# An encoder block in one program: value sums begin with the last key block, and four kinds of small TensorE work are queued behind later dense products

## The chip, the core and the metric

The kernel runs on one core of one Trainium2 chip. The metric is the device time of one execution in microseconds. A core has TensorE (matmuls, called PE in the profile, with weight loads as PEld), VectorE (DVE), ScalarE (ACT), GpSimd (POOL) and SyncE (SP), which here only issues transfers. Each engine works through its own queue in order, and the queues meet in semaphores. All matrix work goes through TensorE; its results land in PSUM banks, from which VectorE and ScalarE read them.

## The reference, cut to what matters

One layer of an encoder over 2048 tokens of width 1024:

```python
h = rms_norm(x, pre_mix_g);  proj = h @ w_in
q, k, v = split(proj[..., :1536])              # 8 heads of 64
y_a = chunk_band_attention(q, k, v, rel_bias)  # chunks of 64, own chunk + 8 before
y_b = rwkv7_time_mix(proj[..., 1536:3328], ...)
merged = sigmoid(gate_a) * (y_a @ proj_a) + sigmoid(gate_b) * (y_b @ proj_b)
x = x + rms_norm(merged @ w_out, post_mix_g)
u = square(relu(rms_norm(x, pre_ffn_g) @ w_up)) @ w_down
x = x + rms_norm(u, post_ffn_g)

# inside rwkv7_time_mix, one step per token:
sa = einsum('bhij,bhj->bhi', state, -kk)
state = state * w + sa[..., None] * (kk * a) + v[..., None] * k
y = einsum('bhij,bhj->bhi', state, r)
# then a group norm of y, "+ bonus", and "* (sigmoid(cg) @ g2)", the gate product
```

Everything is in float32. The order in which the attention sums its key blocks is not fixed by the reference.

## The kernel before, in words

Each float32 operand is split into a high part that TensorE takes at its fast rate (fp32r) and a low remainder, and a product is three matmuls: high by high, high by low, low by high. `wsplit` and `split` (L69 to L83) do it: a weight block of 512 KB is loaded by SP into a raw buffer, ScalarE casts the high part `whi` (L80), VectorE subtracts to get the low part `wlo` (L81). A raw buffer is loaded again when L81 has read it.

The tokens go through in four groups of 512 (g = 0 to 3). A group has three stages: the time mixing (`phase_rwkv`), the attention (`phase_attention`), and the merge of the branches. The feed-forward part follows, two groups at a time. TensorE's filler everywhere is the dense product `dense`: one column block of `w_in`, 24 matmuls of 128x512, named `psd`. 14 of them make the inputs of the time mixing and 16 the branch gates, so a group's time mixing has 30 (matmuls 0 to 719 of a list `self.dl`), and each head pair of the attention has three, for q, k and v. The attention of a group works through four head pairs.

In the time mixing the heads go in four pairs p = 0 to 3, in two blocks of two. For a block: `rwkv_pre` prepares decays and scores (`ps_A`, `ps_bk`, `ps_bonus`); `rwkv_inverse` forms a triangular inverse `X` on VectorE in 31 steps of two short instructions (L593, L599) and two transposes (L602, L604); `rwkv_blocks` (L624, L632) takes `X` to TensorE; `rwkv_trans` makes a transition matrix per chunk of 64 tokens; and `recurrence` walks over the eight chunks. A chunk of a pair (`rwkv_chunk`) is two state products `ps_st` (L710), two output products `ps_y` (L714), and the new state `ST` on VectorE (L715). Both products read the state of the chunk before. When all chunks are done, `rwkv_post` normalises the output: squares on ScalarE, a sum on VectorE, a power on GpSimd, the product `yn` on VectorE (L733). Its second part transposes `yn` back in two halves (`ps_yt`, L742), evicts them with scale and bias on ScalarE (L744, L747), and multiplies by the gate product `ps_g` (three matmuls). While the second block's `X` steps run on VectorE, TensorE does dense products and the first block's `rwkv_post`.

In the attention, q and k of a head pair are taken from their `psd` banks by ScalarE and VectorE (L904 to L915) into `QA`, `QB` and `KK`; `KK` and `VV` hold the group before too, which SP loads from memory (L896, L897) where g > 0. For each head and each half of the queries there are two query blocks: scores `ps_s` against up to 640 keys in two pieces (L958), a minimum on VectorE (L964), the exponential on ScalarE (L971), transposes `ps_pt` (L977), and their split into `PTh` and `PTl` (L981, L982). The value sum `ps_pv` (L988) then adds twelve matmuls: `PTh` with key blocks kt = 0 to 5, `PTl` with the same. Block kt = 5 is filled by the second query block only, kt = 0 by the first only. The residual of the group before is worked off beside the first head pairs (`residual`, loads `o_prev` and `xr`, L1175).

What sets the order: a scheduler puts the instructions into each engine's queue by the order of the code and by their dependencies. In the time mixing, some TensorE instructions carry a further dependency without a semaphore, "behind matmul number n of the list of dense matmuls": `place` notes the pair and `placed` applies it with `queue_behind`. The numbers stand at the head of the file. The other engines' queues, SP's too, follow from the same schedule.

## Time and profile before

| | us |
|---|---|
| median of 3 timed runs (3223.13 to 3225.56) | 3224.54 |
| span of the profiled execution | 3228.5 |
| TensorE busy in it | 3169.8 |
| VectorE busy | 2239.4 |
| ScalarE busy | 1576.3 |

The span is from the first to the last instruction of one execution, which ran 4.0 us longer than the median. A row of a timeline has the start in us, the length in us, the engine, the line, the operation, what it writes and reads, its shape and how many equal ones are merged; in square brackets stand the idle time ahead of it and what ended it. A wait on TensorE shows as such a bracket.

### The profile page before, as it was taken

To read this page: it belongs to the slowest core of one execution; us is meant where nothing else is said; L and a number is where in the kernel's file an instruction comes from. 1 tells how busy PE (TensorE), PEld (TensorE's weight loads), DVE (VectorE), ACT (ScalarE), POOL (GpSimd) and SP (SyncE) were. 2 spreads that over 40 slices of the span, in tenths; PEclk is the share of its full clock that TensorE was granted. 3 is DMA by queue.
4 is the path that set the end of the run, shared out by engine and by line. 5 is a ranking of instruction groups with operands and counts; after the bars stand their busy time and mean duration, and the time that the engine had idled before them with its cause. 6 is when DMAs were issued, how large, how long until landed. Compare 5 with 4: busy or idle time off the path is not lost. (4 is left out here: it accounts for less than half of the span.)

```text
span 3228.5 us, 49999 instructions
## 1 busy us (share of the span) xinstructions
PE 3169.8 (98%) x18913; PEld 2592.1 (80%) x18913; DVE 2239.4 (69%) x3655; ACT 1576.3 (49%) x2511; POOL 602.6 (19%) x1101
## 2 busy tenths in 40 slices
PE   8999999999999999999999999999999999999998
PEld 6877778877888877888877888888888878888887
DVE  7785666786776785776866775887656668765464
ACT  5435635445744435745434755545543454544343
POOL 2222012132112222102222110121211112210000
PEclk9999999999999999999999999999999999999999
DMA  5345374257574237564336557654787876456565
GB/s 169 86 134 184 125 241 123 71 161 245 170 248 121 82 122 246 177 225 151 95 104 222 167 180 272 202 183 153 279 275 251 284 236 209 159 169 235 196 219 172
DMA packets 432282, 592.54 MB, mean 184 GB/s; under 512 B 25300, under 2 KB 295840, under 8 KB 432040
## 3 DMA queue, kind: packets, MB, share of 16 engines
q1 hardware_dynamic: 373928, 408.94, 40.4%
q0 software_dynamic: 48896, 163.61, 13.8%
q10 hardware_dynamic: 9216, 16.78, 1.4%
q8 instruction: 149, 2.44, 0.3%
q14 instruction: 93, 0.76, 0.1%
HBM read 425.37 MB, written 167.01 MB: 183 GB/s over the span
## 5 line engine op out<-in xcount | busy, mean ns | idle before, releaser
L1438 PE MATMUL ps_dn<-fop 128*128 128x512 f32 x2688 | 611.0, 389 | 0.6 <-DVE fop L81 0.6
L1438 PEld LDWEIGHTS ps_dn<-fop 128*128 128x128 f32 x2688 | 504.3, 188 | 105.3 <-DVE fop L81 1.0
L80 ACT CAST whi<-wraw 128x1024 fp32r<-128x1024 f32 x232 | 243.5, 1049 | 331.6 <-PE psd L90 236.3
L90 PE MATMUL psd<-hh,whi 128*128 128x512 f32 x1344 | 369.0, 402 | 1.1 <-ACT k L373 1.1
L81 DVE TENSOR_TENSOR wlo<-wraw,whi 128x1024 fp32r<-128x1024 f32 x232 | 283.1, 1220 | 121.8 <-ACT whi L80 61.9
L90 PE MATMUL psd<-hh,wlo 128*128 128x512 f32 x1344 | 360.6, 397 | 0.0
L90 PE MATMUL psd<-hl,whi 128*128 128x512 f32 x1344 | 357.8, 396 | 0.0
L90 PEld LDWEIGHTS psd<-hl,whi 128*128 128x128 f32 x1344 | 247.5, 188 | 48.9
L90 PEld LDWEIGHTS psd<-hh,whi 128*128 128x128 f32 x1344 | 245.3, 190 | 50.5 <-ACT k L373 1.6
L90 PEld LDWEIGHTS psd<-hh,wlo 128*128 128x128 f32 x1344 | 246.0, 188 | 48.3
L81 DVE TENSOR_TENSOR fop<-xraw,fop 128x1024 fp32r<-128x1024 f32 x112 | 137.0, 1224 | 175.0 <-ACT fop L80 174.4
L80 ACT CAST fop<-xraw 128x1024 fp32r<-128x1024 f32 x112 | 117.8, 1051 | 246.1 <-PE ps_dn L1438 192.2
L1308 POOL DMA_DIRECT2D xd<-X x192 | 104.1, 543 | 379.2 <-ACT X L1305 313.2
L81 DVE TENSOR_TENSOR fop<-wdraw,fop 128x1024 fp32r<-128x1024 f32 x112 | 136.6, 1220 | 21.8 <-ACT fop L80 21.6
L80 ACT CAST fop<-wdraw 128x1024 fp32r<-128x1024 f32 x112 | 117.6, 1050 | 39.9 <-DMA wdraw<-in_w_down_dram 24.7
L964 DVE CUSTOM_DVE_ANT_0 sc<-bias,ps_s 128x640 f32<-128x640 f32 (+4 forms) x128 | 93.9, 734 | 48.6 <-PE ps_s L958 26.6
L971 ACT ACTIVATE sc<-sc,mn 128x640 f32<-128x640 f32 (+4 forms) x128 | 97.7, 763 | 27.7 <-DVE mn L964 26.2
L982 DVE TENSOR_TENSOR PTl<-ps_pt,PTh 128x640 fp32r<-128x640 f32 (+4 forms) x128 | 94.5, 738 | 24.0 <-ACT PTh L981 22.5
L80 ACT CAST s12h<-s 128x1024 fp32r<-128x1024 f32 x32 | 33.7, 1054 | 154.6 <-PE ps_u L90 154.3
L90 PE MATMUL ps_p<-yh,whi 128*128 128x512 f32 x256 | 101.8, 402 | 4.5 <-ACT yh L80 3.5
L1147 PE MATMUL ps_o<-wlo,mh 128*128 128x512 f32 x256 | 100.8, 394 | 4.4 <-DVE wlo L81 4.4
L981 ACT CAST PTh<-ps_pt 128x640 fp32r<-128x640 f32 (+4 forms) x128 | 79.9, 624 | 48.7 <-PE ps_pt L977 47.7
(369 smaller groups left out, 6853.2 us busy)
## 6 DMA issues: line engine op xcount, KB each, us to landing
wraw<-in_w_in_dram SPq DMA_DIRECT2D x168, 512.0 KB
xraw<-xd SPq DMA_DIRECT2D x112, 512.0 KB
xd<-X POOLq DMA_DIRECT2D x192, 256.0 KB, 5.1
wraw<-in_w_up_dram SPq DMA_DIRECT2D x80, 512.0 KB
wdraw<-wd SPq DMA_DIRECT2D x64, 512.0 KB
wdraw<-in_w_down_dram SPq DMA_DIRECT2D x48, 512.0 KB
gd<-gate ACTq DMA_DIRECT2D x64, 256.0 KB
wd<-cmb POOLq DMA_DIRECT2D x64, 256.0 KB, 4.0
```

The lines of the kernel that those rows point to most:

```text
L80: high = self.high = self.nc.scalar.copy(hi, src)
L81: self.low = self.nc.vector.tensor_tensor(lo, src, hi.bitcast(F32), ALU.subtract).ins
L90: mm.append(nc.tensor.matmul(ps, l, r, start=n == 0, stop=n == last).ins)
L964: least = nc.vector.tensor_tensor_reduce(sc[:, 0:n], bias[:, s0:640], pss[:, c0 : c0 + n], 1.0, 3.0e38, ALU.add, ALU.min, mn,)
L971: nc.scalar.activation(sc[:, 0:n], sc[:, 0:n], AF.Exp, scale=-1.0, bias=mn, accum_out=sm[:, col : col + 1])
L981: nc.scalar.copy(hv, pst[:, 0:nk])
L982: nc.vector.tensor_tensor(lv, pst[:, 0:nk], hv.bitcast(F32), ALU.subtract)
L1147: nc.tensor.matmul(ps[t], l[:, k, ts], r[:, k % 2], start=k == 0 and j == 0, stop=k == KB - 1 and j == 2)
L1308: nc.gpsimd.dma_start(self.xd[q][i // 2][:, i % 2], src)
L1438: nc.tensor.matmul(ps, o[:, l, k, sl], o[:, r, k], start=start and n == 0, stop=stop and n == end)
```

## The change

The value sums take the key blocks in the order 5, 0, 1, 2, 3, 4. The fifth chunk's first state product of pair 0 is put behind dense matmul 503 instead of 494. New tables place the first transpose of each half of `ps_yt` for pairs 1 (behind 588 and 592) and 3 (behind 733 and 737), and the gate product of pair 3 (behind 728). Numbers from 720 on are dense matmuls of the first head pair of the attention, so the notes of pair 3 are applied after that pair, and the list is emptied each time.

```diff
-FIFTH = 494
+FIFTH = 503
+TURNS = {1: (588, 592), 3: (733, 737)}
+GATED = {3: 728}
...
         for ins, n in self.places:
             self.queue_behind(ins, self.dl[n])
+        self.places = []
...
             for j in range(4):
-                nc.tensor.transpose(ps[:, j], yn[:, h * 4 + j], self.ident)
+                mm = nc.tensor.transpose(ps[:, j], yn[:, h * 4 + j], self.ident)
+                if j == 0 and p in TURNS:
+                    self.place(mm, TURNS[p][h])
...
-        self.mm3(ps, [(*(x[:, pc] for x in self.g2), *self.lg)])
+        mm = self.mm3(ps, [(*(x[:, pc] for x in self.g2), *self.lg)])
+        if p in GATED:
+            self.places.append((mm[0], GATED[p]))
...
-                kts = [kt for kt in range(6) if not first or half * 2 + kt >= GT]
+                kts = [kt for kt in (5, 0, 1, 2, 3, 4) if not first or half * 2 + kt >= GT]
...
             for p in range(NP):
                 self.att_pair(g, p, beside)
+                if p == 0:
+                    self.placed()
```

What it does to the queues stands here for three places. Line numbers of the changed file are up to nine higher. The first is TensorE's queue at the fifth chunk of pairs 0 and 1; `ps_st` are state products, `ps_y` output products. Before:

```order
L90 MATMUL psd<-hh,wlo 128x512
L710 MATMUL ps_st<-ST,TQ 64x64 x2
L714 MATMUL ps_y<-ST,TQ 64x64 x2
L710 MATMUL ps_st<-ST,TQ 64x64 x2
L714 MATMUL ps_y<-ST,TQ 64x64 x2
L526 MATMUL ps_bonus<-rh,bones 128x512
```

Now:

```order
L92 MATMUL psd<-hh,wlo 128x512
L717 MATMUL ps_y<-ST,TQ 64x64 x2
L92 MATMUL psd<-hh,wlo 128x512
L717 MATMUL ps_y<-ST,TQ 64x64 x2
L529 MATMUL ps_bonus<-rh,bones 128x512
L540 MATMUL ps_bk<-ident,BK 128x128 x4
L92 MATMUL psd<-hh,wlo 128x512 x3
L529 MATMUL ps_bonus<-rl,bones 128x512
L92 MATMUL psd<-hh,wlo 128x512 x2
L540 MATMUL ps_bk<-ident,BK 128x128 x4
L92 MATMUL psd<-hh,wlo 128x512
L713 MATMUL ps_st<-ST,TQ 64x64 x4
```

The state products of the fifth chunk went behind, the output products of that chunk stayed. The second place is TensorE's queue at the end of k's dense product of the first head pair and at v's, in a group with g > 0; `ps_s` are the first scores. Before:

```order
L90 MATMUL psd<-hh,wlo 128x512 x8
L958 MATMUL ps_s<-KK,QA 128x320
L958 MATMUL ps_s<-KK,QB 128x320
L90 MATMUL psd<-hh,whi 128x512 x8
L90 MATMUL psd<-hl,whi 128x512 x8
L90 MATMUL psd<-hh,wlo 128x512 x8
L958 MATMUL ps_s<-KK,QA 128x320
L958 MATMUL ps_s<-KK,QB 128x320
```

Now:

```order
L92 MATMUL psd<-hh,wlo 128x512 x8
L965 MATMUL ps_s<-KK,QA 128x320
L965 MATMUL ps_s<-KK,QB 128x320
L965 MATMUL ps_s<-KK,QA 128x320
L965 MATMUL ps_s<-KK,QB 128x320
L92 MATMUL psd<-hh,whi 128x512 x8
L92 MATMUL psd<-hl,whi 128x512 x8
L92 MATMUL psd<-hh,wlo 128x512 x8
L965 MATMUL ps_s<-KK,QA 128x320
L965 MATMUL ps_s<-KK,QB 128x320
```

Both pieces of the first scores now stand ahead of v's dense product, and the next query block's right behind it. The third place is SP's queue of transfers there; `bv` belongs to `rwkv_post`, `KK` and `VV` are the old keys and values. Before:

```order
L735 DMA bv<-bvd_456 128x512
L66 DMA wraw<-in_w_in_dram 128x8x128
L735 DMA bv<-bvd_457 128x512
L66 DMA wraw<-in_w_in_dram 128x8x128
L896 DMA KK<-kc_304 128x2x512
L897 DMA VV<-vc_308 128x1024
```

Now:

```order
L738 DMA bv<-bvd_456 128x512
L68 DMA wraw<-in_w_in_dram 128x8x128
L738 DMA bv<-bvd_457 128x512
L68 DMA wraw<-in_w_in_dram 128x8x128 x2
L903 DMA KK<-kc_304 128x2x512
L904 DMA VV<-vc_308 128x1024
```

One more weight load stands ahead of the old keys, and of all that follows them.

## The prediction

> **What bounds the kernel now.** I read the page first, then TensorE's waits, then the timelines of the places that the change touches.

> ```profile
> span 3228.5 us, 49999 instructions
> PE 3169.8 (98%) x18913; PEld 2592.1 (80%) x18913; DVE 2239.4 (69%) x3655; ACT 1576.3 (49%) x2511; POOL 602.6 (19%) x1101
> ```

> TensorE is the bound in every stage: it is idle for 58.7 us of 3228.5. Reordering its queue can therefore only take away waits, or make them. The three that the change goes at stand in the view of waits (total, times, longest):

> ```profile
> PE ps_yt L742 <- ACT yf L747: 8.7, 4, 3.0
> PE ps_st L710 <- DVE ST L715: 4.3, 4, 1.1
> PE ps_g L90 <- DVE yn L733: 1.5, 4, 0.4
> ```

> Each occurs once in each of the four token groups, so 14.5 us are at stake, and what the waits do to the clock. The profiled execution is 4.0 us longer than the median 3224.54 of the runs; I work in its times and carry the difference over.

> **The fifth chunk (FIFTH 494 to 503): 0.** In group 1:

> ```profile
> 663.48 0.33 PE L710 MATMUL ps_st<-ST,TQ 64*64 64x64 f32 x4 [1.07 <-DVE ST L715]
> 663.15 0.47 DVE L715 SCALAR_TENSOR_TENSOR ST<-ps_st,gC,S 128x64 f32<-128x64 f32 x2
> ```

> The state product L710 waits for the chunk's start state, which VectorE writes from 663.15. The output product L714 of the same chunk reads the same state, and no number holds it back: in the new order it stands alone where the two stood, behind the same single `hh,wlo` matmul. It takes over the 1.07 us. I take 0 of 4.3 us (bounds 0 and -4.3). What does move is the rest of the recurrence: the order shows 24 dense matmuls instead of 5 between this place and the last chunk. At 0.227 us (24 of them from 769.97 to 775.41 in the rows on attention below) these 19 are 4.3 us. The recurrence is off the path there; who needs it next is told in the next part.

> **The output transposes of pair 1: -4.8.** The four waits, and the clock in stretches of the trace around them (us, PE busy, PEclk, DMA share, GB/s):

> ```profile
> 221.85 0.63 PE L742 MATMUL ps_yt<-ident,yn 128*64 128x128 f32 x4 [1.91 <-ACT yf L747]
> 694.46 0.63 PE L742 MATMUL ps_yt<-ident,yn 128*64 128x128 f32 x4 [2.02 <-ACT yf L747]
> 1192.76 0.64 PE L742 MATMUL ps_yt<-ident,yn 128*64 128x128 f32 x2 [2.99 <-ACT yf L747]
> 1696.18 0.63 PE L742 MATMUL ps_yt<-ident,yn 128*64 128x128 f32 x4 [1.82 <-ACT yf L747]
> ```

> ```profile
> 219.08:222.49 3.41, 1.50 (x9) 1.00 0.65 204
> 222.49:225.90 3.41, 3.41 (x11) 0.50 0.92 266
> 1191.88:1195.29 3.41, 2.53 (x11) 0.50 0.93 276
> 1195.29:1198.70 3.41, 3.41 (x10) 0.50 0.33 102
> 1693.65:1697.06 3.41, 1.59 (x10) 1.00 0.74 232
> 1697.06:1700.47 3.41, 3.34 (x17) 1.00 0.89 250
> ```

> Beside the wait, a stretch of 3.41 us in which TensorE was busy for only 1.50 us is followed by one at half clock (1.7 us lost); one with 1.59 us busy is not. So group 0 pays 1.9 + 1.7 = 3.6 us, group 1 2.0, group 2 3.0 + 3.4 = 6.4, group 3 1.8: 13.8 in all. The transposes now stand 12 dense matmuls (2.7 us) later, past all but the end of the longest wait. But TensorE then runs into the next thing that VectorE owes it, the inverse X of the next block of pairs, for which L624 is queued:

> ```profile
> 233.39 1.19 DVE L602 STREAM_TRANSPOSE X<-X 128x512 f32<-128x512 f32 x1
> 236.98 1.20 PE L624 MATMUL ps_t<-X,NA 32*32 32x32 f32 x64
> 705.90 1.17 DVE L602 STREAM_TRANSPOSE X<-X 128x512 f32<-128x512 f32 x1
> 708.24 0.95 PE L624 MATMUL ps_t<-X,NA 32*32 32x32 f32 x48
> 1205.24 1.18 DVE L602 STREAM_TRANSPOSE X<-X 128x512 f32<-128x512 f32 x1
> 1209.06 1.10 PE L624 MATMUL ps_t<-X,NA 32*32 32x32 f32 x58
> 1707.84 1.17 DVE L602 STREAM_TRANSPOSE X<-X 128x512 f32<-128x512 f32 x1
> 1709.93 1.20 PE L624 MATMUL ps_t<-X,NA 32*32 32x32 f32 x64
> 1201.97 1.23 DVE L81 TENSOR_TENSOR wlo<-wraw,whi 128x1024 fp32r<-128x1024 f32 x1 [1.30 <-PE psd L90]
> ```

> X was ready 2.40, 1.17, 2.64 and 0.92 us before L624 (start of L624 less end of L602): 7.1 us is all that TensorE can gain before it waits there instead. Only in group 2 was VectorE itself held up by TensorE (the last row, 1.30 us), which makes 8.4. From this goes the later recurrence: the normalised output `yn` that opens VectorE's X steps follows the last chunk, which comes 4.3 us later, though VectorE had other work first. I take 0.9 us a group (bounds 0 and 2.5), since most of the shift is covered by that work. So -8.4 + 3.6 = -4.8 (bounds -8.4 and 0), and new waits at L624 of about 2 us (in group 2 about 3).

> **Gate products and transposes of pair 3: -1.5.** The ps_g wait, 0.4 us a group, goes: nine dense matmuls (2 us) now cover it. Bounds 0 and -1.5.

> **What that does to the start of attention: +8.9 and +2.7.** The dense products of attention stood behind those transposes, and the loads behind what those products free. Group 1:

> ```profile
> 764.50 1.23 DVE L81 TENSOR_TENSOR wlo<-wraw,whi 128x1024 fp32r<-128x1024 f32 x1 [1.62 <-PE psd L90]
> 769.68 0.30 PE L958 MATMUL ps_s<-KK,QA 128*128 128x320 f32 x1
> 769.97 1.98 PE L90 MATMUL psd<-hh,whi 128*128 128x512 f32 x8
> 771.19 0.68 DVE L915 TENSOR_TENSOR KK<-psd,KK 64x512 fp32r<-64x512 f32 x1
> 773.25 1.28 DVE L1175 SCALAR_TENSOR_TENSOR xr<-o_prev,rs_p,xr 128x1024 f32<-128x1024 f32 x1
> 775.90 0.82 DVE L964 CUSTOM_DVE_ANT_0 sc<-bias,ps_s 128x640 f32<-128x640 f32 x1 [1.37 <-PE ps_s L958]
> 775.41 0.30 PE L958 MATMUL ps_s<-KK,QA 128*128 128x320 f32 x1
> 758.59 0.59 SPq L896 DMA_DIRECT2D KK<-kc  x1
> 761.27 0.54 SPq L1171 DMA_DIRECT2D xr<-in_x_dram  x1
> ```

> Two things change. In SP's queue the load of old keys (L896, issued at 758.59, 11.1 us ahead of its reader at 769.68) now stands behind one more weight load. That one reuses the buffer which the split at 764.50 empties, so it can't go before 765.73, and the keys about 0.5 us later, at 766.2. How long they take:

> ```profile
> vc<-VV POOLq DMA_DIRECT2D x12, 512.0 KB, 2.9
> 2615.80 6.72 DMA t2l<-td
> ```

> Nothing in the page tells it for this load; 2.9 us (a store of its size) and 6.72 (a load on the chain that ended last) bound it, and I take 5.7, nearer to the load: 771.9, 2.2 us after the reader's turn. In TensorE's queue, the second half of the first scores, which needs the new keys that L915 writes until 771.87, has moved from behind the value product to in front of it, where 769.97 was its turn: 1.9 us, in the same time. So TensorE stands until about 772.0 to 772.3, and the value product with all behind it starts 2.3 us later. Group 0 has no old keys, but the same move:

> ```profile
> 298.60 2.06 PE L90 MATMUL psd<-hh,whi 128*128 128x512 f32 x8
> 299.93 0.69 DVE L915 TENSOR_TENSOR KK<-psd,KK 64x512 fp32r<-64x512 f32 x1
> ```

> 300.62 less 298.60 is 2.0 us. Together 2.0 + 3 x 2.3 = 8.9 (bounds 2.0, which is 0.5 us each, and 11.6, which is 3.2 with the slow load). Then `xr` (761.27) is issued 7.6 us later as well, at 768.9, and lands between 771.8 and 775.6; VectorE's L1175 waits for it, the minimum of the first scores stands behind it, and the next scores wait for that. They are due right behind the value product, 5.4 us after 772.3; 1.28 us of L1175 and 0.82 of the minimum (L964) end between 774 and 778, later if the weight load slows `xr`. I take 0.9 us in groups 1 to 3: +2.7 (bounds 0 and 5.7).

> **The new waits and the clock: +3.5.** The new waits are four at L624 and four at L958, of about 2 us. By the stretches above, 1.9 us of idling inside one stretch costs 1.7 us and less costs nothing; a wait of 2.0 to 2.3 us lies inside one with 1.9 us in about half the places. I take two of eight, 3.4, rounded up (bounds 0 and 8.5). [...]

> **Value sums from the last block: -0.5.** They cost little as it is:

> ```profile
> L988 PE MATMUL ps_pv<-PTh,VV 128*128 128x256 f32 x336 | 67.3, 309 | 0.7
> ```

> Idle before them is 0.7 us in all; the six products now stand together behind one wait. Bounds -0.7 and +3, as later blocks wait for whole sums.

> **Sum.** 0 - 4.8 - 1.5 + 8.9 + 2.7 + 3.5 - 0.5 = +8.3 us: a profiled span of 3236.8, a median of **3232.8**.

> **The rivals.** (1) *The start of attention is covered*: the keys land in 2.9 us and the copies of the new keys run earlier, as VectorE and ScalarE come there sooner, so nothing waits at L958, and X comes no later. For it: 11.1 us of lead in the old queue. Against: the split at 764.50 waited for TensorE itself. It decides at a wait at L958 below 0.5 us. Then -8.4 - 1.5 - 0.5 = -10.4: 3214.1. This is the other side. (2) *A wash*: 1 us at L958 instead of 2.2, nothing at the next scores: -4.8 - 1.5 + 4.0 + 3.5 - 0.5 = +0.7: 3225.2. For it: the same copies that take part in the wait can start as soon as the product ends. (3) *The clock holds*: no new wait fills a stretch, as in group 1 (2.02 us, no loss): +4.8, 3229.3. [...] (4) *Loads pile up*: the slow load (11.6), 1.9 us at the next scores (5.7), three slow stretches (5.1), and X late by 1.35 us (-3.0): -3.0 - 1.5 + 11.6 + 5.7 + 5.1 - 0.5 = +17.4, 3241.9. (5) That the change does what it says, with every wait simply gone, needs VectorE's X and the fifth chunk's output to be early; the rows above exclude it.

> **How the numbers follow.** The forecast has 0.36, rival 1 0.16, rival 2 0.20, rival 3 0.12, rival 4 0.16. About 0.2% (6.4 us) is what a measurement of this kernel can tell from no change. The forecast's own range is 3228 to 3237, of which 0.04 lies within 0.2%. Slower: 0.32 + 0.16 = 0.48; within: 0.04 + 0.12 + 0.20 = 0.36; faster: 0.16. The range goes most of the way to rivals 1 and 4: 3217 to 3241.

> **What would show it.** Right: no wait at L742 (now L745); the wait on ST at the output product (L717) in place of L713, 1.07 us, four times; waits on X at L624's line, 1.5 to 2.5 us, and about 2 us at the first scores of each group's attention; the load of old keys issued after the weight load and within 6 us of its reader. Wrong: the wait on ST gone; less than 0.5 us at L624's line, which would mean that VectorE has more room than its X rows say; old keys landed before their reader; or a clock of 0.50 behind waits shorter than 1.5 us.

## The result and the profile after

The changed kernel takes 3237.16 us (median of 9 runs, 3231.15 to 3242.96), the kernel before 3225.78 in the same series (9 runs, 3223.13 to 3230.85). The ratio is 1.0031, with a 95% interval of 1.0023 to 1.0039: 10 us slower by the ratio (11.4 by the medians), in the forecast's direction and inside its range. That the sum came out so well is in part luck: as will be seen, terms that were sized too small stood on both sides of it and about cancelled.

The profiled execution has a span of 3233.1 us, 4.6 more than the one of before. The one of before was above its median and the new one below its own, so differences read from these two traces are smaller than the timed one; where it matters, I use the timed ratios. A timed run counts 1.7 us more than the span of the same execution (3234.82 against 3233.1), so by this offset the one profiled before ran 5.7 us above its first median, not 4.0. The forecast carries that difference on both sides, and its +8.3 doesn't depend on it.

The head of the page and TensorE's waits in the changed kernel (total, times, longest):

```profile
span 3233.1 us, 50017 instructions
PE 3168.6 (98%) x18913; PEld 2595.4 (80%) x18913; DVE 2237.1 (69%) x3655; ACT 1572.4 (49%) x2511; POOL 599.9 (19%) x1101
...
PE ps_t L627 <- DVE X L605: 5.5, 5, 1.3
PE psd L92 <- DVE QA L914: 4.5, 4, 1.6
PE ps_pt L984 <- DVE VV L935: 4.2, 3, 1.4
PE ps_y L717 <- DVE ST L718: 4.2, 4, 1.1
PE ps_s L965 <- DMA KK<-kc: 3.6, 2, 1.8
PE ps_s L965 <- DVE KK L922: 2.9, 2, 1.4
```

The waits for the transposes (8.7 us) and for ps_g (1.5) are gone, and so is the one at the state product. In their place stand a wait on the state at the output product and one on X at L627, and at the start of attention each group waits at its first scores and again at the value product, v's dense product (for `QA`). Where the time went is seen best if each group is cut at three places of TensorE's queue that are in both kernels: the first `ps_ug` (L674), behind the first block's X products, the second block's X products (L624, now L627), and the first `ps_vt` of the attention. From the X products to the first `ps_vt`, in stretches of the trace (us, busy of PE, PEld, DVE, ACT, POOL, PEclk, DMA share, GB/s), before:

```profile
236.98:304.97 67.99, 67.39 (x779) 53.63 (x778) 37.57 (x66) 30.27 (x55) 18.43 (x37) 1.00 0.62 204
708.24:776.38 68.14, 67.51 (x781) 54.06 (x780) 39.96 (x69) 31.55 (x58) 21.91 (x45) 1.00 0.72 239
1209.06:1277.22 68.16, 67.52 (x782) 54.06 (x781) 38.53 (x67) 30.12 (x56) 20.85 (x43) 1.00 0.71 240
1709.93:1778.08 68.15, 67.53 (x781) 54.06 (x781) 40.20 (x69) 31.80 (x58) 21.82 (x44) 1.00 0.71 238
```

and after:

```profile
235.63:307.93 72.30, 69.07 (x781) 55.06 (x781) 39.89 (x71) 32.30 (x59) 19.84 (x38) 0.98 0.59 194
707.97:782.37 74.40, 71.54 (x784) 56.96 (x784) 42.11 (x72) 32.86 (x59) 22.06 (x43) 0.95 0.66 222
1210.65:1284.18 73.53, 70.21 (x784) 55.95 (x784) 41.94 (x72) 32.85 (x59) 22.06 (x43) 0.98 0.66 227
1712.27:1785.27 73.00, 70.15 (x784) 55.88 (x785) 42.02 (x72) 32.85 (x59) 21.38 (x42) 0.98 0.67 227
```

This is the loss: 4.3, 6.3, 5.4 and 4.9 us, 20.8 in all. PEclk tells that five half-clock stretches of 3.41 us lie in it (two in group 1), which cost 1.7 us each, 8.5 together. Before the X products, in the stage where VectorE works on X, the change gains 6.3 us: the four groups took 90.88, 89.64, 93.13 and 89.40 us and now take 89.2 each; 5.1 of it are three half-clock stretches that are no longer there. How much of this is the change is open: variants 2, 3 and 9 below leave this stage as it was and take 359.3 to 362.9 us there in all, before 363.1, the change 356.8. So the gain lies between 2.5 and 6.3 us by the execution that is compared. From the first `ps_vt` to the merge, the four groups are 5.0 us shorter (0.9 to 1.6 each). The remaining stretches are 4.8 us shorter in all; in the profiles of the variants they are shorter by 1.3 to 4.7 us too, whatever was changed, so I give that to no edit.

Group 1 at the start of attention, in the changed kernel's timeline:

```profile
765.55 1.23 DVE L83 TENSOR_TENSOR wlo<-wraw,whi 128x1024 fp32r<-128x1024 f32 x1 [4.72 <-PE psd L92]
767.30 0.59 SPq L903 DMA_DIRECT2D KK<-kc  x1
771.26 0.68 DVE L922 TENSOR_TENSOR KK<-psd,KK 64x512 fp32r<-64x512 f32 x1 [1.87 <-ACT KK L921]
772.38 0.39 PE L965 MATMUL ps_s<-KK,QA 128*128 128x320 f32 x1 [1.82 <-DMA KK<-kc]
773.19 0.69 DVE L914 SCALAR_TENSOR_TENSOR QA<-psd,QA 64x512 fp32r<-64x512 f32 x1
774.03 3.65 PE L92 MATMUL psd<-hh,whi 128*128 128x512 f32 x8 [0.83 <-DVE QA L914]
777.61 1.28 DVE L1184 SCALAR_TENSOR_TENSOR xr<-o_prev,rs_p,xr 128x1024 f32<-128x1024 f32 x1 [1.86 <-DMA xr<-in_x_dram]
779.61 1.05 ACT L82 CAST whi<-wraw 128x1024 fp32r<-128x1024 f32 x1 [5.48 <-issue]
783.68 1.15 ACT L1189 ACTIVATE o_prev<-xr,rs_r 128x1024 f32<-128x1024 f32 x1 [1.36 <-POOL rs_r L139]
784.74 0.24 ACT L934 CAST VV<-ps_vt 128x128 fp32r<-128x128 f32 x1
788.03 0.74 PE L984 MATMUL ps_pt<-ident,sc 128*128 128x128 f32 x5 [1.41 <-DVE VV L935]
```

The chain is the one that was forecast as far as the scores: the split ends at 766.78, the old keys are asked for at 767.30, and TensorE waits 1.82 us for them. In group 2 it is the same (1.76); in group 3 the new keys come last (1.43), as in group 0, which has no old ones (1.45). The next two links were not forecast. The value product, right behind, waits another 0.83 us for a bank that still holds q, since the second half of q is copied only at 773.19, and its eight matmuls, 1.98 us before, take 3.65 at half clock (0.50 from 774.15). And `xr`, late by its load, doesn't delay the next scores. It is ScalarE that comes late: its work on `xr` (L1187 and L1189) stands ahead of the copies of V, and for those the first `ps_pt` waits 1.41 us. But `xr` is ready at 778.89, and what holds ScalarE is a weight cast that now stands ahead of L1187 in its queue and starts only at 779.61, just after the value product's `hl,whi` matmuls have ended (779.53); before, L1187's counterpart L1178 stood ahead of the cast. In groups 1 to 3 L1187 starts 1.7 to 2.3 us after `xr` is ready, which is more than the wait. The profile doesn't name what the cast waited for.

### The profile page after: what moved, and what is told of

Its sections match the earlier page's. It is cut to its first block, busy times and chain, and to the rows that moved or that the text cites. A ratio compares the mean times of both kernels' runs of the same rounds, so it can differ in the third digit from the quotient of the medians.

```text
span 3233.1 us, 50017 instructions
## 1 busy us (share of the span) xinstructions
PE 3168.6 (98%) x18913; PEld 2595.4 (80%) x18913; DVE 2237.1 (69%) x3655; ACT 1572.4 (49%) x2511; POOL 599.9 (19%) x1101
## 3 DMA queue, kind: packets, MB, share of 16 engines
q0 software_dynamic: 48896, 163.61, 13.8%
## 5 line engine op out<-in xcount | busy, mean ns | idle before, releaser
L988 ACT CAST PTh<-ps_pt 128x640 fp32r<-128x640 f32 (+4 forms) x128 | 79.9, 624 | 51.2 <-PE ps_pt L984 50.3
## 6 DMA issues: line engine op xcount, KB each, us to landing
wraw<-in_w_in_dram SPq DMA_DIRECT2D x168, 512.0 KB
xraw<-xd SPq DMA_DIRECT2D x112, 512.0 KB
wraw<-in_w_up_dram SPq DMA_DIRECT2D x80, 512.0 KB
wdraw<-wd SPq DMA_DIRECT2D x64, 512.0 KB
wdraw<-in_w_down_dram SPq DMA_DIRECT2D x48, 512.0 KB
```

Of the source, the lines that this page charges most:

```text
L988: nc.scalar.copy(hv, pst[:, 0:nk])
```

## The experiments

Eleven variants were timed, in three series. Those of one series share the runs of before, whose medians were 3227.94 (variants 1 to 4), 3227.83 (5 to 8) and 3228.54 (9 to 11).

| variant | median us | ratio to before | 95% interval |
|---|---|---|---|
| the change | 3237.16 | 1.0031 | 1.0023 to 1.0039 |
| 1: change without transposes of pair 3 | 3222.00 | 0.9982 | 0.9973 to 0.9991 |
| 2: transposes of pair 3 alone | 3246.82 | 1.0053 | 1.0041 to 1.0066 |
| 3: order of value sums alone | 3223.81 | 0.9987 | 0.9978 to 0.9996 |
| 4: as 1, FIFTH 494 | 3217.88 | 0.9968 | 0.9955 to 0.9980 |
| 5: change, old keys loaded first | 3244.74 | 1.0052 | 1.0038 to 1.0065 |
| 6: change, q copied first | 3229.49 | 1.0006 | 0.9997 to 1.0015 |
| 7: as 4, transposes of pair 3 at 724 | 3215.99 | 0.9961 | 0.9947 to 0.9974 |
| 8: as 4, transposes of pair 3 at 728 | 3226.39 | 0.9992 | 0.9984 to 1.0001 |
| 9: whole sums alone | 3219.97 | 0.9976 | 0.9967 to 0.9985 |
| 10: as 7, whole sums, old block order | 3212.12 | 0.9954 | 0.9941 to 0.9966 |
| 11: FIFTH 503 alone | 3224.23 | 0.9990 | 0.9981 to 0.9999 |

### Which edit costs: variants 1 and 2

```diff
-TURNS = {1: (588, 592), 3: (733, 737)}
+TURNS = {1: (588, 592)}
```

> The change without the transposes of pair 3 behind 733 and 737; the rest stays (FIFTH 503, TURNS of pair 1, GATED, value sums). Theory 1, the prediction's sizes: the start of attention is as before, 3225.8 - 4.8 (pair 1) - 1.5 (gate products) - 0.5 (value sums) + 1.7 (one slow stretch at L627) = about 3220.7. Theory 2, the sizes that the trace of the changed kernel shows by stretch (before to the first L624 of the second block -6.3, first ps_vt to first ps_o -5.0, that is the value sums, ps_g -1.5 to -2.4): 3225.8 - 6.3 - 5.0 - 2 = about 3212.5. Rival, that the late recurrence of FIFTH is what delays the start of attention: it stays long, above 3232.

Variant 2 is the kernel before with only this:

```diff
+TURNS = {3: (733, 737)}
```

> Before with only the transposes of pair 3 behind 733 and 737. Theory 1, the prediction's sizes: start of attention 8.9 + 2.7, one to two slow stretches 1.7 to 3.4: 3225.8 + 14 = about 3240. Theory 2, by the stretches from L627 to the first ps_vt in the trace of the changed kernel (4.3, 6.3, 5.4, 4.9, together 20.8, of which 8.5 are half clock): 3225.8 + 16 to 21 = 3242 to 3247. Rival, that the gate product of pair 3 or the recurrence is needed for the loss: within 3 us of before.

The loss is in the transposes of pair 3 and nowhere else. Without them the stretch of group 1 from the X products to the first `ps_vt` is even shorter than before, with them alone it is as long as in the whole change (variant 1, then variant 2):

```profile
706.56:774.09 67.53, 67.30 (x781) 54.15 (x781) 40.97 (x70) 31.91 (x58) 22.58 (x45) 1.00 0.72 239
```

```profile
712.47:787.15 74.68, 71.45 (x785) 56.72 (x784) 41.06 (x71) 32.56 (x59) 21.80 (x43) 0.95 0.66 227
```

Over the four groups variant 2 loses 21.5 us there, and 17 us by its ratio. The rivals, that the later recurrence or the gate product is needed for it, are out. Variant 1 is 5.9 us faster than before: nearer to the prediction's sizes (-5.1) than to those read from the two traces (-13). For these I had counted every half-clock stretch of one profiled execution of before as if all executions had them, and the 5.0 us from the first `ps_vt` to the merge, which variant 1's own trace doesn't show (642.2 us against 641.4 before).

### A step at one load: variants 7 and 8

```diff
-FIFTH = 503
+FIFTH = 494
-TURNS = {1: (588, 592), 3: (733, 737)}
+TURNS = {1: (588, 592), 3: (724, 728)}
```

> As the variant without FIFTH 503 and without transposes of pair 3, but with these transposes behind 724 and 728. The one weight load is still behind the old keys in SP's queue. Theory 1, that the loss comes by the order of the loads and not by the transposes' own lateness: as the variant without them, about 0.9968 of before, 3217. Theory 2, that the loss grows with each dense product put ahead of the transposes (24 matmuls cost 21.5 us in the kernel with these alone): half of it, 10 us more.

```diff
-TURNS = {1: (588, 592), 3: (724, 728)}
+TURNS = {1: (588, 592), 3: (728, 732)}
```

> The same with the transposes behind 728 and 732, four dense matmuls (0.9 us) later than in the kernel of the same job. Here a second weight load stands ahead of the old keys in groups 1 to 3. Theory 1 (the order of the loads): a step, 3.5 us and a slow stretch (1.7) more from L627 to the first ps_vt in each of the groups 1 to 3, nothing in group 0; 10 to 15 us over the kernel with 724. Theory 2 (lateness alone): 0.9 us a group more, 3 to 4 us over the kernel with 724, group 0 included.

Four dense matmuls (0.9 us) further cost 10.4 us, and the load of the old keys is what changes. In group 1, SP's load and its reader with 724 (variant 7):

```profile
755.67 0.59 SPq L903 DMA_DIRECT2D KK<-kc  x1
766.13 0.30 PE L965 MATMUL ps_s<-KK,QA 128*128 128x320 f32 x1
```

and with 728 (variant 8), where a second weight load stands ahead:

```profile
755.58 7.45 SPq L68 DMA_DIRECT2D wraw<-in_w_in_dram  x2
763.14 0.65 SPq L903 DMA_DIRECT2D KK<-kc  x1
768.91 0.38 PE L965 MATMUL ps_s<-KK,QA 128*128 128x320 f32 x1 [2.17 <-DMA KK<-kc]
```

SP is held at the weight load until its buffer is free, the keys go out 7.5 us later, and a lead of 10.5 us turns into a wait of 2.17. The stretch to the first `ps_vt` is longer by 4.2, 3.5 and 3.0 us in groups 1 to 3 and by 0.6 in group 0, which has no old keys; in groups 1 and 2 1.7 us of it is a half-clock stretch that begins at the X products, ahead of the load's reader, so the load itself is worth at most 1.8 to 3.0 us a group. Here the order of the first scores on TensorE is the same in both kernels, so the late keys alone were enough. With 724 the transposes of pair 3 cost nothing that can be measured (0.9961 against 0.9968 without them). The load is not all of the loss at 733, though: the change is 0.0049 (16 us) over variant 1, variant 8 only 0.0024 (8 us) over variant 4. At 733 the second half of the first scores stands ahead of the value product too, and the copies come later; the next two variants go at those.

### Mending the start of attention: variants 5 and 6

Variant 5 puts the load of old values, and with it that of the keys, ahead of the weight load:

```diff
-        self.nc.sync.dma_start(raw, src)
+        self.raw_load = self.nc.sync.dma_start(raw, src).ins
...
-            nc.sync.dma_start(VV[:, 0].bitcast(F32), self.vc[p])
+            old = nc.sync.dma_start(VV[:, 0].bitcast(F32), self.vc[p]).ins
...
         ps = self.dense(ATT0 + 2 * HW + p * P)
+        if p == 0 and not first:
+            self.queue_behind(self.raw_load, old)
```

> The change, with the loads of the old keys and values ahead of the weight load for v's dense product of the first head pair in SP's queue (groups 1 to 3). Theory 1, that the late old keys are the larger part of the loss at the start of attention: no wait on the load at L967 any more, L629 to the first ps_vt in groups 1 to 3 back to within 1.5 us of before's 68.15, and the whole 8 us or more under the changed kernel. Theory 2, that the late evictions of q and k by ScalarE and VectorE (behind the late transposes) hold TensorE as long as the keys do: that stretch stays 2 us or more longer than before in each group, the wait at L967 is on the new keys then, and the whole is within 5 us of the changed kernel, on either side, since the weights come later instead.

The keys are early (issued at 751.63 in group 1), the wait on their load is gone, and the kernel is some 7 us slower than the change by the ratios. Waits of variant 5, and the cast that they stand on first in group 1:

```profile
PE psd L92 <- ACT whi L82: 9.2, 6, 1.6
PE ps_s L967 <- DVE KK L922: 5.2, 4, 1.4
...
773.22 1.04 ACT L82 CAST whi<-wraw 128x1024 fp32r<-128x1024 f32 x1
```

The second half of the first scores now waits for the new keys, as the prediction said it would at the same time, and the value product waits for its weights: they are loaded in time, but their cast now stands behind the copies of q and k in ScalarE's queue (773.22; in the change such a cast ran at 763.54). So the old keys can't be called the cause alone: take them out, and the late copies hold TensorE almost as long (1.3 us on average against 1.8). From the X products to the first `ps_vt` variant 5 takes 294.0 us in all, the change 293.2. The 7 us are lost behind that, and by this edit's own doing: three of the six waits for weights, 1.44 us each, stand at the next dense product, with two half-clock stretches. Theory 2 had the mechanism, but not the size: I expected at most 5 us either way.

Variant 6 leaves the loads and mends the copies:

```diff
             act = nc.scalar.copy(KK[rw, par, 1], ps[rw])
+            if p + par == 0:
+                self.queue_behind(act.ins, self.emptied[-1][0].ins)
```

> The change, with the copies of the new keys on ScalarE behind both copies of q (in the change, the second half of q is copied after the first half of the keys), first head pair, all groups. In group 0 there are no old keys to load. Theory 1, that the order of the copies makes the second new wait there (1.6 us at the value product, for q's bank): group 0 from L629 to the first ps_vt falls from 72.3 to about 69, with no half clock there (1.7 of it); groups 1 to 3 stay near 73 to 74.4, since the old keys still land late. The whole: 3 to 4 us under the changed kernel. Theory 2, that the copies are late because the transposes are: group 0 stays above 71.

Group 0, where there is no old key to wait for, is almost as before (67.99), and at full clock:

```profile
235.21:303.93 68.72, 67.25 (x778) 53.74 (x778) 39.72 (x69) 31.71 (x57) 19.84 (x38) 1.00 0.62 204
```

So of the 4.3 us of group 0, 3.6 came from the order in which ScalarE copied q and the keys, half of that by the clock. With this hint the first scores of group 0 stand behind the value product again, so copies and scores are mended together here and can't be told apart. Groups 1 to 3 keep 3.6 to 4.1 us, a little under the 4.9 to 6.3 expected: in groups 1 and 2 the old keys are still late (2.20 and 1.85 us), in group 3 the scores wait 1.62 us behind a weight cast. The whole gains 0.25% on the change, 8 us, more than the 3 to 4 expected.

### The fifth chunk: variants 11 and 4

Variant 11 is before with one number changed:

```diff
-FIFTH = 494
+FIFTH = 503
```

> Before with only FIFTH 503. The prediction: 0, since the wait of 1.07 us goes over to the output product; the later recurrence can cost 0.9 us a group only where the transposes of pair 1 no longer wait for something else, so here within 2 us of before. By the difference between the two variants without transposes of pair 3 (0.9982 and 0.9968): up to 4 us slower. In the trace: wait on ST at L717, 1.05 us four times; wait at L745 for the transposes about as before (8 us), since yn and X only come later.

This was the surprise. The wait on the state went to the output product, as forecast; but the waits at the transposes of pair 1 vanished too, though these stand where they stood (behind dense matmuls 576 and 578). Waits of variant 11:

```profile
PE ps_t L627 <- DVE X L605: 5.7, 5, 1.3
PE ps_y L717 <- DVE ST L718: 4.2, 4, 1.1
```

The transposes had waited for a bank that ScalarE evicts. In before, group 1, the eviction stood behind a weight cast that waited 5 us for VectorE:

```profile
691.75 1.05 ACT L80 CAST whi<-wraw 128x1024 fp32r<-128x1024 f32 x1 [5.01 <-DVE T L593]
693.29 0.55 ACT L744 ACTIVATE yf<-ps_yt,cst 64x256 f32<-64x256 f32 x1
```

and in variant 11 no more:

```profile
688.35 1.06 ACT L82 CAST whi<-wraw 128x1024 fp32r<-128x1024 f32 x1 [2.94 <-PE psd L92]
690.76 0.55 ACT L749 ACTIVATE yf<-ps_yt,cst 64x256 f32<-64x256 f32 x1
```

With the recurrence later, the schedule put VectorE's and ScalarE's instructions in another order. The stage before the X products took 89.15 us in each group: just what the whole change has (89.2). On top of FIFTH 503, then, the transposes of pair 1 bring nothing in that stage. Variant 11 gains 6.4 us there on the profile of before, yet 3 us in all by the ratio: from the X products to the first `ps_vt` it takes 4.6 us longer than before, 3.4 of them by half-clock stretches that begin at the X products in groups 0 and 1.

Variant 4 is variant 1 with 494 again:

```diff
-FIFTH = 503
+FIFTH = 494
```

> The change without FIFTH 503 (494 again) and without the transposes of pair 3: TURNS of pair 1, GATED and value sums. By the prediction, in which the later recurrence takes 0.9 us a group from the gain of pair 1: 3.6 us under the kernel that has FIFTH 503 and no transposes of pair 3. Wait at the L627 line below 0.5 us, wait on ST at the state product as before. Rival, that X comes no earlier with 494: the same time within 1 us and the same waits of 1.3 us at the L627 line.

It is 4.1 us under variant 1, where 3.6 was expected. The same stage in variant 4, groups 0 and 3, shows that it comes from there (variant 1 has 89.16 to 89.20):

```profile
146.12:234.51 88.39, 85.43 (x756) 68.98 (x755) 65.23 (x160) 33.61 (x61) 22.75 (x36) 1.00 0.35 112
...
1609.57:1697.96 88.39, 85.47 (x757) 68.98 (x756) 65.21 (x160) 33.61 (x61) 22.77 (x36) 1.00 0.35 112
```

0.8 us a group: the price of the later recurrence, through VectorE's X. The intervals of the two ratios overlap, but the other kernels bear the stage out: with the transposes of pair 1 moved, the four with 494 (variants 4, 7, 8, 10) take 88.4 us a group, once 89.0, and the four with 503 (the change, 1, 5, 6) 89.1 to 89.2. My figure for the wait at L627 was wrong: I expected under 0.5 us, and 1.1 us is left. X sets the end of this stage in both.

### The value sums: variants 3, 9 and 10

```diff
-                kts = [kt for kt in range(6) if not first or half * 2 + kt >= GT]
+                kts = [kt for kt in (5, 0, 1, 2, 3, 4) if not first or half * 2 + kt >= GT]
```

> Before with only the value sums begun with the last key block. Theory 1, the prediction's size: -0.5, 3225.3, not to be told from before. Theory 2, that the 5.0 us which the stretches from the first ps_vt to the first ps_o lost in the changed kernel are theirs: 3221. Under theory 2 the groups 1 to 3 get 1 to 2 us each there, and group 0 less than 1.

The order of the sums alone gains 4.1 us (0.9987), not 0.5; groups 1 and 2 are 2.0 and 1.7 us shorter between the first `ps_vt` and the merge, groups 0 and 3 0.8 us longer. It hardly had a wait to take away. What it takes away is seen in `ps_pv` itself. Groups of instructions, before and then variant 3 (busy us, mean ns, idle before):

```profile
L988 PE MATMUL ps_pv<-PTh,VV 128*128 128x256 f32 x336 | 67.3, 309 | 0.7
L988 PE MATMUL ps_pv<-PTl,VV 128*128 128x256 f32 x336 | 60.2, 288 | 0.0
```

```profile
L995 PE MATMUL ps_pv<-PTh,VV 128*128 128x256 f32 x336 | 55.3, 296 | 0.3
L995 PE MATMUL ps_pv<-PTl,VV 128*128 128x256 f32 x336 | 52.6, 288 | 0.0
```

The busy time falls from 127.5 to 107.9 us with the same matmuls, because they overlap each other more when they stand together (six take 0.95 us in one row, 0.36 and 0.86 in two, as shown below): the mean length of one hardly changes. This is more than the gain, since such a row also counts time in which its matmuls overlap with others. TensorE's busy time as a whole tells the size. Less 1.7 us for every half-clock stretch up to 3180 us, it is 3162.6 us on average in the three kernels with the old sums (before, variants 2 and 11), 3159.2 in the eight with the new order, and 3154.2 in variants 9 and 10, which follow. A single kernel lies up to 3 us off its average, but the 3.4 and 8.4 us less are about what was timed for variants 3 and 9.

Before, the first of a sum often stood alone; in the changed kernel six stand in a row (timelines of TensorE, before and then the changed kernel):

```profile
785.33 0.36 PE L988 MATMUL ps_pv<-PTh,VV 128*128 128x256 f32 x1
787.92 0.86 PE L988 MATMUL ps_pv<-PTh,VV 128*128 128x256 f32 x5
```

```profile
792.20 0.95 PE L995 MATMUL ps_pv<-PTh,VV 128*128 128x256 f32 x6
```

Whether it is the standing together or the block that comes first, variant 9 tells: the old order of blocks, but the first product of a sum behind the last split.

```diff
-                    nc.vector.tensor_tensor(lv, pst[:, 0:nk], hv.bitcast(F32), ALU.subtract)
+                    low = nc.vector.tensor_tensor(lv, pst[:, 0:nk], hv.bitcast(F32), ALU.subtract)
...
-                    nc.tensor.matmul(pv[:, half], st, x[:, kt], start=i == 0, stop=i == len(terms) - 1)
+                    mm = nc.tensor.matmul(pv[:, half], st, x[:, kt], start=i == 0, stop=i == len(terms) - 1)
+                    if i == 0:
+                        self.queue_behind(mm.ins, low.ins)
```

> Before, key blocks in the old order 0 to 5, but a value sum's first matmul is put behind the last split of the weights (VectorE's PTl of the second query block). By the order of TensorE's queue the 672 value products then stand in 106 unbroken rows; in before in 176, in the variant with only the new key order in 125; changes from one tile to another on TensorE 1619, 1730 and 1648. Theory 1, that the new key order gains by fewer changes between kinds of matmul, whatever the order of the blocks: 111 changes fewer against 82, so 4.1 x 111 / 82 = about -5.6, 3222; ps_pv's own busy time at or under the 108 us of that variant. Theory 2, that it gains since the fresh block is summed first: no gain here, or a loss by waits for the splits, 3228 or more.

It gains 0.24%, 8 us, without any new block order: theory 1. Its `ps_pv` rows are at 51.2 (`PTh`) and 58.0 us. By the counts in the expectation, 82 changes of tile less gave 4.1 us and 111 less gave 7.7, so one change between kinds of matmul costs some 50 to 70 ns (an estimate from these two variants; their intervals are wide enough that the two don't differ).

Variant 10 puts whole sums into variant 7, in place of the new block order:

> The kernel with pair 3 at 724 and 728 and FIFTH 494, with the old key order and the whole sums of the other kernel of this job in place of the new key order. If the parts add: 3216 less about 1.5 us more from the sums, 3214. If the sums and the earlier attention ask for the same time of ScalarE and VectorE: no better than 3216.

3212.12 us: the parts add. It is 15 us under before and 25 under the change as it was made, and it does the same kinds of moves: transposes of pair 1 at 588 and 592, of pair 3 at 724 and 728, the gate product at 728, sums undivided; FIFTH stays at 494.

## Why the prediction was right, and where it was not

**The bound and the direction**: right. TensorE stayed at 98%, and the waits taken away came back as others. But "Reordering its queue can therefore only take away waits, or make them" was too narrow: the order also changed how long the same matmuls kept TensorE busy (`ps_pv` 107.9 us in variant 3 for 127.5).

**The fifth chunk, 0**: the wait moved to the output product as said (4.2 us, four times 1.05). But the step priced only that wait and the later chunks. FIFTH alone also took the waits off the transposes of pair 1, by the order of ScalarE's queue, and gained 0.10% (interval 0.01 to 0.19). The order of that queue was there to read; I read TensorE's. The shift of the last chunk was too small as well: 4.3 us counts the 19 dense matmuls alone, but more of the `ps_A` products now stand ahead too, and in group 1 the chunk comes 7.6 us later (13.7 us behind the fifth for 6.1).

**The transposes of pair 1, -4.8**: mechanism and cap right, credit wrong. X is the cap: variant 4, without the later recurrence, gains 9.4 us in that stage on the profile of before, for a cap of 8.4. The change gains 6.3 there, with 3.6 us (0.9 a group) for the later recurrence against 4.1 timed and 0.8 a group by the stage. But with FIFTH 503 the transposes' own move is worth nothing in that stage, and the waits at L627 are 1.3 us, not 2.

**Gate products, -1.5**: the wait is gone; in groups 0 and 1 of variant 1, where nothing else disturbs that stretch, it is 0.6 us a group.

**The start of attention, +8.9 and +2.7**: the place, the load and its times were right (keys asked for at 767.30 for a forecast 766.2; there within 5.1 us for 5.7). The sum was short. Without the clock the four stretches lost 12.3 us, and some 2 more if the gain on ps_g is taken out: 14 against 11.6. The wait at the scores is 6.5 us, less than 8.9. What I had left out is the copy of q behind that of the keys (4.5 us at the value product); and the +2.7 for `xr` at the next scores didn't come at all; in its place stand 4.2 us at `ps_pt`, behind a weight cast that had moved ahead of ScalarE's work on `xr`.

**The clock, +3.5**: undersized, 8.5 from the X products to the first `ps_vt`, 6.8 of it at the start of attention. I applied "1.9 us of idling inside one stretch costs 1.7 us and less costs nothing" to each wait by itself, but in group 1 two waits, of 1.82 and 0.83 us, lie in one stretch (770.74 to 774.15, 0.94 us busy) with half clock behind it. And beside the X products this failed altogether: the stretch of group 1 with the wait of 1.29 us at L627 (705.89 to 709.30, 2.12 us busy) was followed by half clock. I had named a half clock behind waits under 1.5 us as a sign of error, and it came.

**The value sums, -0.5**: the term that failed by most. "They cost little as it is: idle before them is 0.7 us" reads only waits. The cost stood in the busy time, as changes between kinds of matmul, and was worth 4.1 us.

The terms that were too small on the loss side (clock, copies of q) and on the gain side (value sums) about cancelled, and that is luck. **The rivals**: "covered" fell, with waits of 1.4 to 1.8 us at L965 in every group; "a wash" fell with the same waits and those behind them, "the clock holds" with the five half-clock stretches; "loads pile up" came nearest on the clock (5.1 us, where 8.5 came) and had `xr` late, but its cost at the next scores and X wrong. That the change loses lies in two numbers that are a little too far, 733 and 737 at the transposes of pair 3.

## What to carry to other kernels

An order constraint on one engine's queue is an edit of all queues when a scheduler sets the rest: compare every queue, transfers first, and look for a load that has fallen behind one which waits for a buffer. A position a few matmuls further can be free or cost 10 us, so such numbers are tried in both directions and one by one; here one part carried the whole loss (17 us alone) and hid what the others gained together (6 us). On an engine that is busy 98%, look into the busy time too: the same matmuls took less of it here in unbroken rows (`ps_pv` 107.9 us for 127.5).

## What the runs showed of the hardware

```profile
1774.26:1777.67 3.41, 1.55 (x7) 1.26 (x8) 2.83 (x5) 2.71 (x4) 0.00 (x0) 1.00 0.95 374
1777.67:1781.08 3.41, 3.41 (x9) 2.63 (x8) 1.91 (x2) 0.00 (x0) 0.00 (x0) 0.50 1.03 410
```

So 1.86 us of idling in one stretch went with half clock here, and not in one piece: TensorE waits 1.43 us there at 1774.89 and again up to 1776.93.

**Beside the X products, half clock came at more busy time too.** These are matmuls of 32x32. In the two traces 32 stretches at full clock hold 0.6 us or more of them; one, in the changed kernel, was followed by half clock, with 2.12 us of busy time, 1.20 of it X products. The others have 2.63 us or more. Another stretch of the changed kernel has as much busy time, 0.41 us of it X products, and stayed at full clock:

```profile
705.89:709.30 3.41, 2.12 (x69) 1.62 (x68) 3.17 (x9) 0.61 (x1) 0.58 (x1) 1.00 0.53 154
709.30:712.71 3.41, 3.41 (x9) 2.66 (x9) 3.34 (x4) 2.47 (x5) 2.57 (x5) 0.50 0.32 61
...
1207.65:1211.06 3.41, 2.10 (x34) 1.48 (x33) 3.13 (x10) 0.00 (x0) 0.00 (x0) 1.00 0.50 146
1211.06:1214.47 3.41, 3.41 (x62) 2.91 (x57) 3.38 (x5) 2.63 (x5) 3.01 (x5) 1.00 0.10 18
```

In variant 4 a stretch with 2.30 us (702.88 to 706.30, 70 matmuls) was followed by half clock, in variant 7 one with 2.43 us (1694.82 to 1698.23, 70 matmuls) was not. Why stretches with nearly the same busy time differ the runs don't show. The nine executions of the changed kernel spread over 12 us, with a mean clock of 0.995 to 0.997, lowest in the slowest; which stretches lay at half clock is known for the profiled one alone.
